# Turned queries laid out by token halves: two transfers per swapped copy in a hybrid attention layer

## The chip, the cores and the metric

The kernel runs on one core of a Trainium2 chip. The metric is the device time of one execution in microseconds (us); times of a kernel are given as the median of several runs. A profile of one execution shows every instruction on the core's engines: PE (TensorE, matmuls; PEld is its weight load), DVE (VectorE), ACT (ScalarE), POOL (GpSimd) and SP (SyncE, which here issues every data transfer, DMA, of the kernel's loop).

## The reference

One encoder layer is applied to two request groups (prompt and sample, 1024 tokens of 1024 channels each) with the same weights. Cut to what matters here:

```python
qa = rms_norm(qa.reshape(B, S, HQ_A, HEAD_DIM), qn_a)      # 8 heads of 64
ka = rms_norm(ka.reshape(B, S, HKV_A, HEAD_DIM), kn_a)     # 2 heads of 64
...                                                        # rotary positions on both
oa = gqa_attention(qa, ka, va) * jax.nn.silu(za)           # branch A: softmax(q k / 8) v

qb = rms_norm(qb.reshape(B, S, H_B, 2, HEAD_DIM), qn_b)    # 4 heads, two maps of 64 each
kb = rms_norm(kb.reshape(B, S, H_B, 2, HEAD_DIM), kn_b)
...
ob = diff_attention(qb, kb, vb, lam)                       # (softmax map 0 - lam * softmax map 1) v
ob = rms_norm(ob, subln_g) * (1.0 - lam_init)
ob = ob.reshape(B, S, BR_B) * jax.nn.silu(zb)

pa = jnp.einsum('bse,ed->bsd', oa, w_proj_a)
pb = jnp.einsum('bse,ed->bsd', ob, w_proj_b)
merged = jax.nn.sigmoid(ga) * pa + jax.nn.sigmoid(gb) * pb
out = jnp.einsum('bsd,de->bse', merged, w_out)
return x + gate[:, None, :] * out                          # gate from c and w_ada
```

## The kernel before

**Numbers in two parts.** TensorE reads rounded float32. A turned query or key (channels on partitions, tokens along the row) is therefore kept as 128 partitions: 64 hold the rounded values, the other 64 what rounding left. A score is the sum of two products: the query as it lies with the key (L743, rounded with rounded and rest with rest), and the query with its two partition halves exchanged (L744, the mixed terms). The exchanged copy is the tile `sw`, which `swapped` (L612 to L620) makes by DMA, since a DMA can move data between partitions. The turning and splitting is `pairs_T` (two transposes on TensorE, L593; ACT writes the rounded half, L595; DVE the rest, L596).

**Units.** Attention works in units of 256 queries (`pr`, the quarter of the tokens) by two score maps: two heads in branch A, the two maps of a head in branch B. A group has 16 units of A (two halves of four heads) and 16 of B, so there are 64. A unit has one `sw` copy and four score steps of 128 queries (`scores`, `softmax_unit`): four matmuls into one of two score banks, the row maximum on DVE (L745), exp on ACT (L746). `flip` then combines the two maps (B only, L786), transposes 32x32 blocks on DVE (L787) and sends the block by four DMAs to the tile `q` (L796, "q<-p" in the profile; the queries themselves are "u" there). The values read `q`: L802 for A, L819 for B. Their output goes to DRAM (L811, L827, "od<-oo").

**Stages of a group.** A head makes A's keys, values and the first half of its queries (`kva_gen`, `qa_gen`), woven with gate columns `z` (L709, written by L722, "zd<-ev"). Then come six phases. In phase 0 attention over A's first half runs beside `qa_gen` of the second; in phase 1 the second half beside B's values and the first B head's queries and keys (`qkb_gen`); in phases 2 to 5 a B head each, beside the next head's `qkb_gen`; the last phase runs beside `gate_gen` (first group only; its eight loads L474 are of 512 KB, into four free 1 MB buffers), the rest of z, and the merge. Merges and the output projection follow.

**What sets the order.** `weave` mixes attention with the fill by hand-set weights; a scheduler then orders each engine's instructions by priorities and its own estimate of when each can start. Attention has a raised priority. A unit's copy `sw` is asked for with the first score steps of the unit before (`attention`, L842 and on), in a pool with two buffers. All DMAs stand in one queue, that of SP, in the order the scheduler gave; their completions rotate over 8 semaphores. Queries, keys, weights and hidden states share 15 buffers of 128 x 2048 numbers (`utile`).

Before the change a unit's queries are two tiles (heads m = 0, 1), each with 1024 tokens for two head pairs; `swapped` has four transfers of 64 partitions x 256 tokens, one for each map and half.

Of the kernel before, what the change touches and what calls it, by code (L numbers as in the profile page):

```python
# [12 lines left out]
F32 = mybir.dt.float32  # L13
F32R = mybir.dt.float32r
# [6 lines left out]
P = 128  # L21
# [67 lines left out]
def kernel(ctx: ExitStack, tc: tile.TileContext, t: dict):  # L89
    nc = tc.nc  # L90
# [36 lines left out]
    def utile():  # L127
        return upool.tile([P, 2048], F32R, tag="u", name=nm("u"))
# [21 lines left out]
    def mtile(tag, shape, dt=F32, bufs=None):  # L150
        return mpool.tile(shape, dt, tag=tag, name=nm(tag), bufs=bufs)
# [4 lines left out]
    dma = nc.sync.dma_start  # L156
# [427 lines left out]
    LO, HI = slice(0, 64), slice(64, 128)  # L584

    def pairs_T(x3, even, odd):


        nb = x3.shape[1] // 2
        ps = gbank()[:, : nb * P].rearrange("p (b n) -> p b n", b=nb)  # L590
        x = x3.rearrange("p (b two) d -> p b (two d)", two=2)
        for b in range(nb):
            nc.tensor.transpose(ps[:, b, :], x[:, b, :], ident)  # L593
        for dst, hi, lo in ((even, LO, HI), (odd, HI, LO)):
            nc.scalar.activation(dst[hi], ps[hi], AF.Copy)  # L595
            nc.vector.tensor_tensor(out=dst[lo], in0=ps[hi], in1=dst[hi].bitcast(F32), op=ALU.subtract)  # L596
# [14 lines left out]

    def swapped(u):  # L612

        qs = u["q"]
        sw = mtile("sw", [P, 2, 256], F32R)[:, : len(qs)]
        sl = slice(u["pr"] * 256, u["pr"] * 256 + 256)
        for m, q in enumerate(qs):
            for a, b in ((LO, HI), (HI, LO)):
                dma(sw[a, m].bitcast(F32), q[b, sl].bitcast(F32))
        return sw  # L620


# [1 line left out]

    def v2(u):
        return u.rearrange("p (h n) -> p h n", h=2)

    def kva_gen(ht, out):
        w = kva_w.pop()[0] if kva_w else load_w(w_cols(w_in, (C_KA, 256)))
# [18 lines left out]

    def qa_gen(st, half):
        w = load_w(w_cols(w_in, (C_QA + half * 256, 256)))  # L650
        qs = [v2(utile()), v2(utile())]
        ht = st["ht"]
        st["qa"][half] = qs

        def front(tt, ps):
            e = by_turns(tt)
            x3, s3 = rms(ps, 4, e)
            e.tensor_tensor(out=x3, in0=x3, in1=gqa.unsqueeze(1).to_broadcast([P, 4, HD]), op=ALU.mult)
            rope(x3, s3, st["cosA"][:, tt], st["sinA"][:, tt], 16, e)
            return x3  # L660

        def back(tt, x3):
            sl = slice(tt * P, (tt + 1) * P)
            pairs_T(x3, qs[0][:, :, sl], qs[1][:, :, sl])
            made[id(qs)] = tt + 1

        yield from pipelined(ht, w, front, back)

    def qkb_gen(ht, out, h):
        w = load_w(w_cols(w_in, (C_QB + h * P, P), (C_KB + h * P, P)))  # L670
        qk = out[h] = (v2(utile()), v2(utile()))

        def front(tt, ps):
            e = by_turns(tt)
            x3, s3 = rms(ps, 4, e)
            x4 = x3.rearrange("p (a m) d -> p a m d", a=2)
            e.tensor_tensor(out=x4, in0=x4, in1=gB.unsqueeze(2).to_broadcast([P, 2, 2, HD]), op=ALU.mult)
            rope(x3[:, :, :16], s3[:, :, :16], cosB[:, tt], sinB[:, tt], 8, e)
            return x3

        def back(tt, x3):
            sl = slice(tt * P, (tt + 1) * P)
            pairs_T(x3, qk[0][:, :, sl], qk[1][:, :, sl])
            made[id(qk)] = tt + 1

        yield from pipelined(ht, w, front, back)
# [50 lines left out]
    def softmax_unit(q, sw, k, pt, su):  # L737

        m = tiny.tile([P, 1], F32, tag="m", name=nm("m"))
        s = sbank()  # L740
        for n in range(2):
            sl = slice(n * 512, (n + 1) * 512)
            nc.tensor.matmul(s[:, sl], q, k[:, sl], start=True, stop=False)  # L743
            nc.tensor.matmul(s[:, sl], sw, k[:, sl], start=False, stop=True)  # L744
        nc.vector.tensor_reduce(out=m, in_=s, axis=AX.X, op=ALU.max, negate=True)  # L745
        nc.scalar.activation(  # L746
            pt.rearrange("p (j c a) -> p j c a", j=4, c=8), s.rearrange("p (c a j) -> p j c a", c=8, j=4),
            AF.Exp, bias=m, accum_out=su,
        )

    def scores(u, i):

        pairs = "h" not in u
        t, m = (i % 2, i // 2) if pairs else (i // 2, i % 2)
        qt = u["pr"] * 2 + t
        if "sw" not in u:
            u["sw"] = swapped(u)
        pt = ptile()
        if pairs:
            su = u["su"][:, m, qt : qt + 1]  # L760
        else:
            su = u["su"][:, qt : qt + 1] if m == 0 else tiny.tile([P, 1], F32, tag="su", name=nm("su"))
        softmax_unit(u["q"][m][:, qt * P : (qt + 1) * P], u["sw"][:, m, t * P : (t + 1) * P], u["k"][m], pt, su)
        if pairs:
            u[m, t] = [pt]
            return m, t
        if m == 0:
            u[t] = [pt]
        else:
            f = tiny.tile([P, 1], F32, tag="r", name=nm("r"))  # L770
            nc.vector.reciprocal(f, su)
            nc.gpsimd.tensor_scalar(
                out=f, in0=f, scalar1=u["su"][:, qt : qt + 1], scalar2=nlam, op0=ALU.mult, op1=ALU.mult
            )
            u[t] += [pt, f]
        return (0, t) if m else None
# [238 lines left out]
    def units_of(st):  # L1015

        def a_unit(half, b, pr):
            kv = half
            j = half * 4 + 2 * b
            return {  # L1020
                "q": [st["qa"][half][i][:, b] for i in range(2)], "k": [st["ka"][:, kv]] * 2,
                "v": st["va"][:, :, kv, :],
                "pr": pr, "od": st["od"][j // 2], "su": st["suA"][:, j : j + 2],
            }

        def b_unit(h, pr):
            qk = st["qkb"][h]
            return {
                "q": [qk[m][:, 0] for m in range(2)], "k": [qk[m][:, 1] for m in range(2)],
                "v": st["vb"][h], "pr": pr, "h": h,  # L1030
                "od": st["od"][4 + h], "ss": st["ssB"], "su": st["suB"][:, h],
            }

        def there(kind, n, pr):
            return made.get(id(st[kind].get(n)), 0) > 2 * pr + 1

        units = []
        for half in range(2):
            units += [
                (half, lambda a=(half, b, pr): a_unit(*a), lambda a=("qa", half, pr): there(*a))  # L1040
                for b in range(2) for pr in range(4)
            ]
        for h in range(4):
            units += [
                (2 + h, lambda a=(h, pr): b_unit(*a), lambda a=("qkb", h, pr): there(*a)) for pr in range(4)
            ]
        return units
# [22 lines left out]
    for g in range(2):  # L1070
        st = states[g]
# [108 lines left out]
```

## Time and profile before

| | before |
|---|---|
| median of 3 runs | 1943.93 us (1940.35 to 1944.71) |
| profiled execution | 1944.48 us |
| its span | 1942.7 us |
| mean granted TensorE clock | 0.987 |
| PE / DVE / ACT / POOL busy | 1867.0 / 1137.7 / 760.3 / 724.5 us |
| `sw` transfers, KB each, median us to landing | 256, 64.0, 2.1 |
| q<-p transfers, KB each, median us to landing | 768, 128.0, 2.6 |

The busy row says how long each engine ran an instruction within the span; DMA issues on SP are not counted in it. A row of the timeline gives start, duration, engine, line, operation, output and inputs with their shape and count; in brackets stands the idle time before it and what ended that. A row of a tile gives the durations as min/median/max in ns and the first and last start. "To landing" is the time from the start of an issue to the completion. The granted clock is the share of full speed that TensorE got.

### The profile page before, as it was taken

Reading aid. Unit: us, or ns where it says so; the run is one execution under the profiler, and the core shown is the slowest. Engines: PE = TensorE matmul, PEld = TensorE weight load, DVE = VectorE, ACT = ScalarE, POOL = GpSimd, SP = SyncE. Lnnn points to the kernel's source line nnn. Section 1 sums busy time; section 2 is a strip of 40 time slices with the busy share of each in tenths; the row PEclk is TensorE's granted clock in tenths of the full one; section 3 lists DMA queues with packets and bytes.
Section 4 is the critical chain, followed back from the end, with each engine's and each line's share of the span. In section 5 each row is a group of like instructions: output and inputs, shape, how many; then the busy total and the mean of one; then the engine's idle time right before and its main releaser. Section 6 shows DMA issues by size and latency. Waiting matters only on the chain. (4 is left out here: it accounts for less than half of the span.)

```text
span 1942.7 us, 29466 instructions
## 1 busy us (share of the span) xinstructions
PE 1867.0 (96%) x10434; PEld 1566.8 (81%) x10434; DVE 1137.7 (59%) x1613; ACT 760.3 (39%) x1548; POOL 724.5 (37%) x1008
## 2 busy tenths in 40 slices
PE   6889999999999998999999899999999999999999
PEld 4777778888888996788888677888888788877887
DVE  5767752444667366757455676445447736666731
ACT  4534442444445344324233444334445534442210
POOL 2564321433456254121336343124456616422110
PEclk9999999999999999999999899999999999999999
DMA  8126774546243355875531567655524423587531
GB/s 315 62 80 166 190 197 129 155 127 201 80 136 102 102 164 155 271 253 187 198 104 51 160 173 195 172 158 152 164 76 139 115 77 93 152 250 251 169 103 54
DMA packets 268882, 295.02 MB, mean 152 GB/s; under 512 B 35136, under 2 KB 217536, under 8 KB 268736
## 3 DMA queue, kind: packets, MB, share of 16 engines
q1 hardware_dynamic: 268736, 293.15, 51.0%
q8 instruction: 83, 1.36, 0.3%
q14 instruction: 63, 0.52, 0.1%
HBM read 133.59 MB, written 42.01 MB: 90 GB/s over the span
## 5 line engine op out<-in xcount | busy, mean ns | idle before, releaser
L709 PE MATMUL f<-u,w 128*128 128x512 f32 x2256 | 588.3, 397 | 2.5 <-ACT w L192 1.0
L709 PEld LDWEIGHTS f<-u,w 128*128 128x128 f32 x2256 | 414.5, 189 | 87.4 <-issue 3.1
L539 PE MATMUL f<-w,u 128*128 128x256 f32 x3456 | 482.4, 285 | 2.4 <-DVE ev L719 1.1
L539 PEld LDWEIGHTS f<-w,u 128*128 128x128 f32 x3456 | 454.6, 191 | 24.7 <-issue 2.7
L745 DVE TENSOR_REDUCE m<-s 128x1 f32<-128x1024 f32 x256 | 310.3, 1217 | 220.3 <-PE s L744 218.2
L746 ACT ACTIVATE p<-s,m 128x1024 f32<-128x1024 f32 x256 | 285.1, 1114 | 290.1 <-DVE m L745 215.2
L194 POOL TENSOR_TENSOR w<-st,w 128x512 fp32r<-128x512 f32 x168 | 222.6, 1342 | 461.3 <-ACT w L192 439.7
L787 DVE STREAM_TRANSPOSE p<-p 128x1024 f32<-128x1024 f32 x192 | 237.7, 1241 | 68.5 <-ACT p L746 56.6
L560 POOL TENSOR_TENSOR rs<-ss,nhalf 128x4 f32<-128x4 f32 (+1 forms) x112 | 111.5, 996 | 312.6 <-DVE ss L559 280.1
L744 PE MATMUL s<-u,sw 128*128 128x512 f32 x512 | 204.7, 401 | 0.0
L192 ACT ACTIVATE w<-st 128x512 fp32r<-128x512 f32 x196 | 114.6, 626 | 148.2 <-DMA st<-in_w_in_dram 92.8
L819 PE MATMUL a<-q,u 128*128 128x256 f32 x512 | 133.8, 396 | 8.1 <-DMA q<-p 5.6
L946 PE MATMUL f<-u,w 128*128 128x512 f32 x552 | 136.8, 398 | 4.0 <-DVE u L957 3.0
L946 PEld LDWEIGHTS f<-u,w 128*128 128x128 f32 x552 | 103.9, 190 | 26.2 <-DVE u L957 3.7
L802 PE MATMUL a<-q,u 128*64 128x256 f32 x1024 | 119.2, 385 | 5.7 <-DMA q<-p 5.7
L819 PEld LDWEIGHTS a<-q,u 128*128 128x128 f32 x512 | 99.5, 200 | 25.6 <-issue 7.0
L743 PE MATMUL s<-u 128*128 128x512 f32 x256 | 108.5, 424 | 10.7 <-ACT p L746 9.9
L596 DVE TENSOR_TENSOR u<-f,u 64x256 fp32r<-64x256 f32 (+1 forms) x196 | 80.6, 411 | 64.4 <-ACT u L595 59.4
L744 PEld LDWEIGHTS s<-u,sw 128*128 128x128 f32 x512 | 97.6, 191 | 17.7 <-issue 0.8
L802 PEld LDWEIGHTS a<-q,u 128*64 128x64 f32 x1024 | 75.3, 138 | 43.9 <-issue 11.4
L743 PE MATMUL s<-u,u 128*128 128x512 f32 x256 | 104.1, 409 | 6.0 <-ACT p L746 4.8
L977 PE MATMUL f<-u,w 128*128 128x512 f32 x456 | 105.6, 389 | 0.0
(169 smaller groups left out, 1984.4 us busy)
## 6 DMA issues: line engine op xcount, KB each, us to landing
q<-p SPq DMA_DIRECT2D x768, 128.0 KB, 2.6
st<-in_w_in_dram SPq DMA_DIRECT2D x132, 256.0 KB, 3.1
zd<-ev SPq DMA_DIRECT2D x96, 256.0 KB, 2.6
sw<-u SPq DMA_DIRECT2D x256, 64.0 KB, 2.1
p<-zd SPq DMA_DIRECT2D x64, 256.0 KB, 3.8
u<-in_w_ada_dram SPq DMA_DIRECT2D x8, 1024.0 KB, 11.6
od<-oo SPq DMA_DIRECT2D x64, 128.0 KB, 2.5
st<-in_w_in_dram SPq DMA_DIRECT2D x64, 128.0 KB, 2.9
```

The lines of the kernel that those rows point to most:

```text
L192: nc.scalar.activation(wh, st, AF.Copy)
L194: e.tensor_tensor(out=wl, in0=st, in1=wh.bitcast(F32), op=ALU.subtract)
L539: ins = nc.tensor.matmul(ps, lt[c][:, sl], w[:, c, wi, :], start=(k == 0), stop=(k == 23))
L709: ins = nc.tensor.matmul(ps, w[:, c, wi, e * P : (e + 1) * P], rt[c], start=(k == 0), stop=(k == 23),)
L743: nc.tensor.matmul(s[:, sl], q, k[:, sl], start=True, stop=False)
L744: nc.tensor.matmul(s[:, sl], sw, k[:, sl], start=False, stop=True)
L745: nc.vector.tensor_reduce(out=m, in_=s, axis=AX.X, op=ALU.max, negate=True)
L746: nc.scalar.activation(pt.rearrange("p (j c a) -> p j c a", j=4, c=8), s.rearrange("p (c a j) -> p j c a", c=8, j=4), AF.Exp, bias=m, accu ...
L787: nc.vector.transpose(pt, pt)
L802: lambda k=k, m=m: nc.tensor.matmul(acc[(LO, HI)[m]], u["v"][:, k], pT[m][:, k], start=(k == 0), stop=(k == 7))
L819: nc.tensor.matmul(acc, u["v"][:, k], pT[:, k], start=(k == 0), stop=(k == 7))
L946: nc.tensor.matmul(ps, w[:, c, wi, d * P : (d + 1) * P], o[:, oi, :], start=(k == 0), stop=(k == 11))
```

## The change

Queries, and B's keys, are now laid out by token halves. `by_tokens` takes the same two buffers, but each holds 512 tokens of both maps, as [partition, head pair b, map m, 512 tokens]; `tokens_of` gives the slices of one 128-token tile to `pairs_T`. In a unit all 256 queries of both maps thus lie in one buffer, and `swapped` moves both maps at once: two transfers of 64 partitions x 2 maps x 256 tokens (128 KB) in place of four of 64 x 256 (64 KB). `softmax_unit` gets the key as a list of two halves of 512 columns, which is how its matmuls already read it. The number of instructions on PE, DVE, ACT and POOL and the buffers stay the same. Line numbers behind L620 shift: L619 to L618, L709 to L714, L743/L744 to L748/L749, L745/L746 to L750/L751, L786/L787 to L792/L793, L796 to L802, L802 to L808, L819 to L825, L827 to L833.

```diff
     def swapped(u):
 
-        qs = u["q"]
-        sw = mtile("sw", [P, 2, 256], F32R)[:, : len(qs)]
-        sl = slice(u["pr"] * 256, u["pr"] * 256 + 256)
-        for m, q in enumerate(qs):
-            for a, b in ((LO, HI), (HI, LO)):
-                dma(sw[a, m].bitcast(F32), q[b, sl].bitcast(F32))
+        sw = mtile("sw", [P, 2, 256], F32R)
+        sl = slice(u["pr"] % 2 * 256, u["pr"] % 2 * 256 + 256)
+        q = u["q"][u["pr"] // 2]
+        for a, b in ((LO, HI), (HI, LO)):
+            dma(sw[a].bitcast(F32), q[b, :, sl].bitcast(F32))
         return sw
...
+    def by_tokens():
+
+        return [utile().rearrange("p (b m n) -> p b m n", b=2, m=2) for _ in range(2)]
+
+    def tokens_of(ts, tt):
+        sl = slice(tt % 4 * P, (tt % 4 + 1) * P)
+        return [ts[tt // 4][:, :, m, sl] for m in range(2)]
...
-        qs = [v2(utile()), v2(utile())]
+        qs = by_tokens()
...
-            sl = slice(tt * P, (tt + 1) * P)
-            pairs_T(x3, qs[0][:, :, sl], qs[1][:, :, sl])
+            pairs_T(x3, *tokens_of(qs, tt))
...
-        qk = out[h] = (v2(utile()), v2(utile()))
+        qk = out[h] = by_tokens()
...
-            sl = slice(tt * P, (tt + 1) * P)
-            pairs_T(x3, qk[0][:, :, sl], qk[1][:, :, sl])
+            pairs_T(x3, *tokens_of(qk, tt))
...
-            nc.tensor.matmul(s[:, sl], q, k[:, sl], start=True, stop=False)
-            nc.tensor.matmul(s[:, sl], sw, k[:, sl], start=False, stop=True)
+            nc.tensor.matmul(s[:, sl], q, k[n], start=True, stop=False)
+            nc.tensor.matmul(s[:, sl], sw, k[n], start=False, stop=True)
...
-                "q": [st["qa"][half][i][:, b] for i in range(2)], "k": [st["ka"][:, kv]] * 2,
+                "q": [x[:, b] for x in st["qa"][half]],
+                "k": [[st["ka"][:, kv, n * 512 : (n + 1) * 512] for n in range(2)]] * 2,
...
-                "q": [qk[m][:, 0] for m in range(2)], "k": [qk[m][:, 1] for m in range(2)],
+                "q": [x[:, 0] for x in qk], "k": [[x[:, 1, m] for x in qk] for m in range(2)],
```

The scheduler gives another order with it. Three places follow. The first is SP's queue in the first group where the gate's loads are issued (L474, `u_...<-in_w_ada_dram`), before:

```order
L827 DMA od_135<-oo_7223 128x256
L474 DMA u_7414<-in_w_ada_dram 128x2x512 x2
L722 DMA zd_7292<-ev_7290 128x512
L796 DMA q_7274<-p_7204 128x1x256 x4
L619 DMA sw_7394<-u_6622 64x256 x2
L619 DMA sw_7394<-u_6623 64x256 x2
L474 DMA u_7434<-in_w_ada_dram 128x2x512 x2
L796 DMA q_7274<-p_7295 128x1x256 x4
L827 DMA od_136<-oo_7359 128x256
L216 DMA st_7630<-in_w_in_dram 128x2x256
```

and now:

```order
L833 DMA od_135<-oo_7167 128x256
L727 DMA zd_7234<-ev_7232 128x512
L802 DMA q_7218<-p_7148 128x1x256 x4
L618 DMA sw_7336<-u_6572 64x2x256 x2
L474 DMA u_7297<-in_w_ada_dram 128x2x512 x2
L474 DMA u_7322<-in_w_ada_dram 128x2x512 x2
L474 DMA u_7354<-in_w_ada_dram 128x2x512 x2
L474 DMA u_7374<-in_w_ada_dram 128x2x512 x2
L802 DMA q_7218<-p_7237 128x1x256 x4
L833 DMA od_136<-oo_7301 128x256
L216 DMA st_7568<-in_w_in_dram 128x2x256
```

Four of the eight loads stood further up still, ahead of the row shown first; all eight are now directly ahead of the four transfers of `p_7237` (`p_7295` before). The second place is DVE in the first group at the second B head, where score units (tiles `s`, maxima `m`) run into one another; before:

```order
L745 TENSOR_REDUCE m_6433<-s_6434 128x1
L771 RECIPROCAL r_6366<-su_6357 128x1
L596 TENSOR_TENSOR u_5533<-f_6015,u_5533 64x2x128
L786 SCALAR_TENSOR_TENSOR p_6298<-p_6356,r_6366,p_6298 128x1024
L745 TENSOR_REDUCE m_6464<-s_6465 128x1
L745 TENSOR_REDUCE m_6502<-s_6503 128x1
L787 STREAM_TRANSPOSE p_6298<-p_6298 128x1024
L596 TENSOR_TENSOR u_5532<-f_6062,u_5532 64x2x128
L771 RECIPROCAL r_6472<-su_6463 128x1
```

and now:

```order
L750 TENSOR_REDUCE m_6385<-s_6386 128x1
L777 RECIPROCAL r_6318<-su_6309 128x1
L596 TENSOR_TENSOR u_5491<-f_5971,u_5491 64x2x128
L750 TENSOR_REDUCE m_6416<-s_6417 128x1
L750 TENSOR_REDUCE m_6452<-s_6453 128x1
L792 SCALAR_TENSOR_TENSOR p_6250<-p_6308,r_6318,p_6250 128x1024
L777 RECIPROCAL r_6424<-su_6415 128x1
L750 TENSOR_REDUCE m_6466<-s_6467 128x1
L793 STREAM_TRANSPOSE p_6250<-p_6250 128x1024
```

The combine `p_6250` moved behind two maxima, and one more maximum, which stood behind the second transpose before, moved ahead of the first; on PE three score units now stand in a row, where two did. The third place is PE in the first group's phase 0, at the values of the fourth unit (tile `a`, the last score unit ahead of it is `s_2434`, now `s_2406`); before:

```order
L593 MATMUL f_2265<-ident,row_1978 128x128 x2
L743 MATMUL s_2434<-u_360,u_900 128x512
L744 MATMUL s_2434<-u_360,sw_2183 128x512
L743 MATMUL s_2434<-u_360,u_900 128x512
L744 MATMUL s_2434<-u_360,sw_2183 128x512
L802 MATMUL a_2321<-q_2282,u_361 64x256
```

and now:

```order
L748 MATMUL s_2406<-u_360,u_899 128x512
L749 MATMUL s_2406<-u_360,sw_2173 128x512
L748 MATMUL s_2406<-u_360,u_899 128x512
L749 MATMUL s_2406<-u_360,sw_2173 128x512
L539 MATMUL f_2176<-w_1410,u_530 128x256
L539 MATMUL f_2176<-w_1410,u_531 128x256
L539 MATMUL f_2176<-w_1410,u_530 128x256 x2
L539 MATMUL f_2176<-w_1410,u_531 128x256
L593 MATMUL f_2253<-ident,row_1970 128x128 x2
L808 MATMUL a_2309<-q_2270,u_361 64x256
```

Another unit's score is what stands just ahead of the values before, and fill work now; the values' own last score lies further up in both.

More of the change, by code (lines that the diff above doesn't have):

```diff
@@ L762, in scores @@
             su = u["su"][:, qt : qt + 1] if m == 0 else tiny.tile([P, 1], F32, tag="su", name=nm("su"))
-        softmax_unit(u["q"][m][:, qt * P : (qt + 1) * P], u["sw"][:, m, t * P : (t + 1) * P], u["k"][m], pt, su)
+        q = u["q"][qt // 4][:, m, qt % 4 * P : (qt % 4 + 1) * P]
+        softmax_unit(q, u["sw"][:, m, t * P : (t + 1) * P], u["k"][m], pt, su)
         if pairs:
```

## The prediction

> **What bounds the kernel now.** I read the page first: busy time, the costliest groups (the maximum and the exp of each score unit, which matter below), DMA issues.
>
> ```profile
> PE 1867.0 (96%) x10434; PEld 1566.8 (81%) x10434; DVE 1137.7 (59%) x1613; ACT 760.3 (39%) x1548; POOL 724.5 (37%) x1008
> ...
> L745 DVE TENSOR_REDUCE m<-s 128x1 f32<-128x1024 f32 x256 | 310.3, 1217 | 220.3 <-PE s L744 218.2
> L746 ACT ACTIVATE p<-s,m 128x1024 f32<-128x1024 f32 x256 | 285.1, 1114 | 290.1 <-DVE m L745 215.2
> ...
> q<-p SPq DMA_DIRECT2D x768, 128.0 KB, 2.6
> ...
> sw<-u SPq DMA_DIRECT2D x256, 64.0 KB, 2.1
> ```
>
> TensorE is busy for 1867.0 of 1942.7 us, so 75.7 us of idle is all that any change outside TensorE can take, and an added wait, or a slower clock behind one, is the only way to lose. The change removes no matmul. So the question is which of TensorE's waits the swapped copies stand behind. I read next what TensorE waited for, per releaser (us in total, times, longest):
>
> ```profile
> PE s L743 <- ACT p L746: 14.7, 8, 3.7
> ...
> PE a L802 <- DMA q<-p: 5.7, 3, 2.5
> PE a L819 <- DMA q<-p: 5.6, 1, 5.6
> ```
>
> No wait names `sw`. The transfers q<-p (turned softmax blocks going to the values) are waited for 11.3 us in four places, and they share SP's queue with `sw`. Then the two tiles' own rows: the 256 `sw` transfers of the run, the 36 between 140 and 300 us, and the q<-p between 200 and 290 us (duration of an issue on SP, min/median/max in ns).
>
> ```profile
> L619 SPq DMA_DIRECT2D sw<-u x256: 461/594/1777, 108.9 to 1713.5; - x128
> ...
> L619 SPq DMA_DIRECT2D sw<-u x36: 468/595/1361, 152.2 to 288.8; - x36
> ...
> L796 SPq DMA_DIRECT2D q<-p x90: 542/602/1657, 199.8 to 287.5; - x90
> ```
>
> SP's timeline shows what this does where branch A's first half runs (start, duration, count):
>
> ```profile
> 212.22 0.52 SPq L619 DMA_DIRECT2D sw<-u  x1
> 212.84 1.21 SPq L796 DMA_DIRECT2D q<-p  x2
> ...
> 214.75 1.19 SPq L796 DMA_DIRECT2D q<-p  x2
> 215.98 0.61 SPq L619 DMA_DIRECT2D sw<-u  x1
> 216.69 1.19 SPq L796 DMA_DIRECT2D q<-p  x2
> 217.93 0.60 SPq L619 DMA_DIRECT2D sw<-u  x1
> 218.58 0.60 SPq L796 DMA_DIRECT2D q<-p  x1
> 219.22 0.60 SPq L619 DMA_DIRECT2D sw<-u  x1
> 219.94 3.16 SPq L796 DMA_DIRECT2D q<-p  x5
> ```
> ```profile
> 211.32 1.25 DVE L787 STREAM_TRANSPOSE p<-p 128x1024 f32<-128x1024 f32 x1 [0.74 <-DMA q<-p]
> ```
> ```profile
> 220.53 0.85 PE L709 MATMUL f<-u,w 128*128 128x512 f32 x3
> 221.22 0.88 PE L539 MATMUL f<-w,u 128*128 128x256 f32 x6
> ...
> 222.86 0.40 PE L744 MATMUL s<-u,sw 128*128 128x512 f32 x1
> 225.51 2.77 PE L802 MATMUL a<-q,u 128*64 128x256 f32 x23 [2.25 <-DMA q<-p]
> ```
>
> SP issues with hardly a gap; four `sw` issues of one unit stand among the q<-p. The block turned at 212.57 gets its issues some 4 us later, and TensorE waits 2.25 us for the last. Here, and in the same stretch of the second group (from 1080 us), SP's queue lies on the path. Last, busy times and clock by stretch:
>
> ```profile
> core 0: us, PE busy (x) PEld busy (x) DVE busy (x) ACT busy (x) POOL busy (x), PEclk, DMA share, GB/s
> 140.00:300.00 160.00, 154.75 (x957) 125.33 (x956) 104.06 (x115) 69.56 (x137) 52.42 (x68) 1.00 0.66 179
> ...
> 1080.00:1240.00 160.00, 156.56 (x932) 126.20 (x932) 104.70 (x116) 70.43 (x139) 54.51 (x71) 0.97 0.67 184
> ```
>
> The two stretches leave 5.25 and 3.44 us idle. Elsewhere q<-p is waited for at one place only, the 5.6 us before L819.
>
> **The change part by part.** *Copies.* Each unit issued 4 × 0.594 = 2.38 us on SP; it now issues two, of 128 row pieces each instead of 64. No row shows a copy of that shape. The nearest is q<-p, also 128 KB from SP, at 0.602. Bounds: 2 × 0.461 (the shortest `sw` row) and 2 × 1.19 (an issue that costs by its rows, nothing saved). I take 2 × 0.62 = 1.24, near q<-p, so 1.1 us a unit: 64 units give about 73 us of SP, 9 units × 1.1 = 10 us in 140–300. Outside the two stretches it lies beside TensorE's work and is worth 0; were that cover gone, it would be 1.1 us a unit.
>
> The Trainium skill ("DMA: Bandwidth & Descriptors", Issuing engines are not separate DMA queues) says that the time a sequencer takes to initiate a DMA is usually small relative to the DMA itself, which speaks against any gain. Here the row has 0.594 us against 2.1 us to landing, and on a full queue the issues add up; by the page's rule the two terms below from SP would be 0.
>
> *Stretch 140–300.* The waits are the 2.25 us above and another of 0.9 (of the 5.7 us under L802, 2.25 and the 2.53 below leave that). The queue gets some 10 us lighter. But the order moves too: counted in the two orders and priced by the spacing of the rows above (0.23 us for a 512-column matmul, 0.12 for a 256-column one), TensorE's work between a unit's last score and its values shrinks for units 3 to 8 from 13.2, 16.3, 20.0, 17.3, 17.5, 16.1 us to 8.9, 11.5, 11.3, 13.9, 14.2, 10.9. Most of what the queue gives is thereby asked back. Bounds: −4.3 (both waits and half of the stretch's other 2.1 us) and +6 (four of the six units reach their values 1.5 us before the data). I take −1.6, half of the waits, because the queue and the order move by like amounts.
>
> *Stall at 1166.* SP, TensorE, and the granted clock of the 3.4 us behind (columns as above):
>
> ```profile
> 1159.85 1.84 SPq L619 DMA_DIRECT2D sw<-u  x3
> 1161.79 5.16 SPq L796 DMA_DIRECT2D q<-p  x8
> ```
> ```profile
> 1166.55 3.82 PE L802 MATMUL a<-q,u 128*64 128x256 f32 x20 [2.53 <-DMA q<-p]
> ```
> ```profile
> 616.50:619.90 3.40, 3.40 (x10) 2.66 (x8) 1.70 (x4) 1.83 (x3) 3.40 (x8) 0.50 0.62 167
> ...
> 1166.00:1169.40 3.40, 2.85 (x14) 2.47 (x16) 2.17 (x4) 0.64 (x3) 2.49 (x4) 0.50 0.65 174
> ```
>
> The values wait for the last of eight q<-p that queue behind three `sw` issues. The pair becomes at most one `sw` issue there: the q<-p goes out some 1.2 us earlier, and half of the 2.53 us stays. A half clock over 3.4 us costs 1.7 us more, and whether it comes hangs on the rest of the gap. Bounds −4.2 (both gone) and 0; I take −2, about the middle.
>
> The Trainium skill ("TensorE: Matmul & The Clock Gate", Part 1) says that the clock is halved after an idle window of some 3.4 us and gaps below some 3 us should keep it warm. The lengths agree (3.4 and 6.8 us at 0.50), but 2.53 us of idle was enough here and 2.25 us at 225 was not. By the page's rule these 1.7 us would not hang on this gap and the term would be −1.2.
>
> *Five score units in a row at 1078.* Two banks hold scores; a third unit waits for the first's maximum (L745, 1.22 us) and exp (L746, 1.11 us).
>
> ```profile
> 1082.93 0.79 PE L743 MATMUL s<-u,u 128*128 128x512 f32 x1 [0.85 <-ACT p L746]
> ```
>
> The new order puts the fifth unit behind two transposes and 24 z matmuls, so 0.85 us of waiting goes, and perhaps part of the half clock there. Bounds −0.85 and −2.6 (with 1.7 of clock), I take −1.7, the middle.
>
> *Three score units in a row at 622.* Before, two came, then z. Now a third follows at once. By the rows of L745 and L746 (1217 and 1114 ns) the first unit's maximum and exp end 2.4 us after its last matmul, while the second unit's scores fill 0.95 us: a wait of about 1.5 us. Behind a wait of that size the half clock may follow, as it did from 616.5 in the row above; at 0.4 times its 1.7 us the term is +2.2, with bounds +1.5 (no slow clock) and +3.4 (a wait of 1.7 and the slow clock).
>
> *Gate loads at 735.* The eight loads of 512 KB for the gate (L474) stood in three places and now follow one another, directly ahead of the q<-p that TensorE waits 5.56 us for:
>
> ```profile
> 727.53 1.12 SPq L474 DMA_DIRECT2D u<-in_w_ada_dram  x2
> 730.57 2.55 SPq L796 DMA_DIRECT2D q<-p  x4
> ```
> ```profile
> 735.46 5.60 PE L819 MATMUL a<-q,u 128*128 128x256 f32 x16 [5.56 <-DMA q<-p]
> 742.07 0.44 PE L593 MATMUL f<-ident,row 128*128 128x128 f32 x2 [1.00 <-POOL row L582]
> ```
> ```profile
> 738.68 1.26 POOL L194 TENSOR_TENSOR w<-st,w 128x512 fp32r<-128x512 f32 x1 [1.33 <-ACT w L192]
> ```
> ```profile
> GB/s 255 101 108 138 93 67 82 164 293 328 405 410 401 306 235 237 198 207 285 123 179 265 205 257 405 194 56 4 0 0 0 69 168 311 4 0 0 0 0 0
> ```
>
> The last row is that of 726 to 745 us; it peaks at 410 GB/s. Eight loads are 4.19 MB, at that rate 10.2 us; issued from about 725.5 (behind the earlier q<-p) they end near 736, and the q<-p, if served behind them, near 737, 1.5 us later than now. Against it: POOL's L194, which held the two transposes behind the values up (1.33 us of waiting, then 1.26), moves behind the rows that they need, so the waits at 742 go, 1.00 us here and 0.3 before the next pair. I take +1.0, not the bare difference of 0.2, because the q<-p's own issue of 0.6 us stands behind the loads too. Bounds: −1 (the q<-p hardly later, the 1.3 us gone) and +8 (the rate of the slices behind the peak, 235 GB/s: 17.8 us, so the loads end at 743.3 and the q<-p 0.6 later, 8.4 us behind now; less 1.3, and half a slow-clock window more).
>
> *Rest.* The four waits for q<-p above are all there are; the other units' data land in time: 0 ± 2.
>
> **Sum**: −1.6 − 2 − 1.7 + 2.2 + 1.0 = −2.1 us against the profiled execution, 1944.48 us (span 1942.7 and 1.8 around it), so 1942.4. That execution lies 0.55 us above the median 1943.93 of the three runs (1940.35 to 1944.71), so I forecast **1941.8 us**: no change that can be measured. About 0.2%, 3.9 us, is what separates runs of this kernel from no change.
>
> **The rivals.**
>
> *A, faster: the queue was the whole cause.* With 73 us less on SP all waits for q<-p in the two stretches go. For it: SP without gaps, three q<-p waits there. Against it: values asked for earlier. −3.7 in 140–300, −4.2 at 1166, −2.2 at 1083, +2.2 at 622, 0 at 735: −7.9, so 1936.
>
> *B, slower: the gate loads.* One mechanism, the loads ahead of the q<-p at 735, with the price +8 of the bound above. The other terms make −3.1, so it is slower by more than 3.9 us from a delay of 3.9 + 3.1 + 1.3 = 8.3 us on, that is if the q<-p lands after 743.8; with +8, and +2.2 to +3.4 at 622, the time is 1948.8 to 1950. For it: the 5.56 us show that this place is already short of data. Against it: 410 GB/s was reached here.
>
> *C, slower: moved values meet the old queue.* If in 140–300 the queue stays as late as it is while the values come 3 to 9 us earlier, the waits grow by up to the shrinks: 4.3 + 4.8 + 8.7 + 3.4 + 3.3 + 5.2 = 29.7 us. A wait at one unit also delays the next unit's request, so they don't add in full; a third to two thirds, +10 to +20, with the other −0.5: 1953 to 1963. Against it: the queue does get lighter.
>
> *D, nothing: the saving isn't there.* If an issue costs by its rows, two copies take what four took (2 × 1.19), the two SP terms fall away and the rest cancels to within 2 us: about 1944. For it: no row has this shape. Against it: q<-p moves twice the bytes of `sw` at the same 0.60 us.
>
> **How the numbers follow.** Forecast and D together 0.40 (0.30 and 0.10), A 0.36 with all that lies between it and 1940, B 0.18, C 0.06. From these: faster 0.36, same 0.40, slower 0.24. The likeliest is the forecast. The range reaches to 1932 (A, and twice the 2 us of the rest) and to 1951 (B, and 1 us of the rest), and leaves C and the far end of A out, under 2 in 10. The forecast's own range is 1938 to 1946: the sum, and about 4 us either way before A or B begins.
>
> **What would show it.** An `sw` issue near 0.62 us and two a unit, SP's busy time down by about 70 us: the copies' step. An idle time of TensorE in 140–300 near 3.6 us instead of 5.25, with a smaller wait at L808 (the old L802): the stretch; more than 5.25, rival C. The wait near 1166 under 1.5 us and no slow clock behind it; no wait near 1083; a wait of about 1.5 us on exp near 624; and a values wait for q<-p near 735 of 6 to 7 us with the transposes following at once. Above 13.9 us there (5.56 + 8.3), rival B. I am wrong if TensorE's idle total (75.7 us) leaves 70 to 80 us, or if a large wait stands at none of these places.

## The result and the profile after

The changed kernel takes 1944.47 us (median of 20 runs, 1940.49 to 1950.97), the kernel before 1940.38 us in 20 runs beside it (1934.27 to 1946.18): ratio 1.0022, 95% interval 1.0012 to 1.0031. It is 4.1 us slower, where I forecast no change. A second measurement of the changed kernel gave 1.0019 (1.0006 to 1.0031).

How small this is, equal programs show: the kernel before, built and timed apart twice, stood at 1.0013 (1.0003 to 1.0023) and at 0.9992 (0.9979 to 1.0004) to itself. Some 0.1% can thus be scatter between builds; the sign rests on two measurements of the changed kernel, its size only roughly. Also, the profiled execution of before that the prediction was made from (1944.48 us) lay 4.1 us above the median of the 20 runs, and the three runs shown then (median 1943.93) 3.5 above it.

The copies do what they should. The page of the changed kernel, and its rows of the tile `sw`, for the whole run and for 140 to 300 us:

```profile
PE 1858.6 (96%) x10434; PEld 1561.4 (80%) x10434; DVE 1133.1 (58%) x1613; ACT 759.3 (39%) x1548; POOL 723.2 (37%) x1008
...
sw<-u SPq DMA_DIRECT2D x128, 128.0 KB, 2.5
```
```profile
L618 SPq DMA_DIRECT2D sw<-u x128: 590/632/1992, 109.5 to 1705.4; - x128
...
L618 SPq DMA_DIRECT2D sw<-u x18: 630/632/1992, 151.8 to 278.0; - x18
```

An issue takes 0.632 us where a smaller one took 0.594, and there are half as many: 1.26 us a unit instead of 2.38, 71 us of SP in all. In branch A's first half TensorE now hardly idles: in 205 to 275 us it was busy for all 70 us, and in 140 to 300 us for 159.24 of the 160 us, where it was busy for 154.75 before:

```profile
core 0: us, PE busy (x) PEld busy (x) DVE busy (x) ACT busy (x) POOL busy (x), PEclk, DMA share, GB/s
205.00:275.00 70.00, 70.00 (x436) 56.01 (x437) 50.08 (x56) 35.05 (x69) 28.19 (x36) 1.00 0.74 206
```
```profile
140.00:300.00 160.00, 159.24 (x984) 129.34 (x983) 106.27 (x119) 71.93 (x141) 52.59 (x68) 1.00 0.66 181
```

What TensorE waited for in the changed kernel (total, times, longest) shows where that gain went:

```profile
PE s L748 <- ACT p L751: 15.4, 7, 3.7
PE f L593 <- POOL row L582: 12.9, 4, 9.6
...
PE f L952 <- DVE u L963: 4.4, 4, 1.7
...
PE a L808 <- DMA q<-p: 2.6, 2, 1.9
```

In the kernel before, the second and third of these lines read:

```profile
PE f L593 <- POOL row L582: 4.3, 5, 2.2
...
PE f L946 <- DVE u L957: 3.0, 2, 1.7
```

The wait for q<-p before L819 (5.6 us) has become one of the transposes L593 for POOL (9.6 us), and the merge's matmuls L952 wait for DVE 4.4 us, where L946 waited 3.0. TensorE's idle total is 1941.5 - 1858.6 = 82.9 us, above the 70 to 80 us beyond which the prediction called itself wrong.

To add this up I counted each matmul at its median spacing in the trace of before (the time from its start to the next one's), and took, for equal TensorE work done, how much more time than work passed: idle plus slow clock, in us per stage (stage ends on the clock of before). Between rows the differences count; the level of a stage depends on the spacings taken. The waits quoted with each experiment are pieces of these sums.

```
stage, us      205-275  600-650  715-762  762-865  1060-1098  1140-1215
before            4.0      4.4      6.9      6.6      11.4       3.7
before, 2nd       5.4      4.5      6.9      4.9       9.3       0.6
before, 3rd       3.0      4.5      6.8      4.4       9.0       0.4
changed          -0.6      6.1      9.8      8.7       9.8       2.5
changed, 2nd     -0.6      6.0      9.8      9.4       9.7       4.5
difference       -4.7     +1.6     +2.9     +3.7      -0.2      +1.9   of the means
```

The six differences make +5.2 us; the medians differ by 4.1. In the first four stages the rows of the two kernels lie apart. In the last two they overlap, so -0.2 and +1.9 are not shown to be differences of the kernels. The second and third profile of before are those of the runs `b_again` and `b_third` below, the second of the changed kernel that of `a_again`.

### The profile page after: what moved, and what is told of

Its sections match the earlier page's. It is cut to its first block, busy times and chain, and to the rows that moved or that the text cites. A ratio compares the mean times of both kernels' runs of the same rounds, so it can differ in the third digit from the quotient of the medians.

```text
span 1941.5 us, 29325 instructions
## 1 busy us (share of the span) xinstructions
PE 1858.6 (96%) x10434; PEld 1561.4 (80%) x10434; DVE 1133.1 (58%) x1613; ACT 759.3 (39%) x1548; POOL 723.2 (37%) x1008
## 5 line engine op out<-in xcount | busy, mean ns | idle before, releaser
L714 PE MATMUL f<-u,w 128*128 128x512 f32 x2256 | 585.7, 396 | 2.5 <-DVE w L194 1.1
L714 PEld LDWEIGHTS f<-u,w 128*128 128x128 f32 x2256 | 412.7, 188 | 86.8 <-issue 3.8
L750 DVE TENSOR_REDUCE m<-s 128x1 f32<-128x1024 f32 x256 | 309.9, 1218 | 220.6 <-PE s L749 218.2
L751 ACT ACTIVATE p<-s,m 128x1024 f32<-128x1024 f32 x256 | 285.1, 1114 | 292.9 <-DVE m L750 221.0
L793 DVE STREAM_TRANSPOSE p<-p 128x1024 f32<-128x1024 f32 x192 | 237.0, 1239 | 65.4 <-ACT p L751 57.7
L749 PE MATMUL s<-u,sw 128*128 128x512 f32 x512 | 204.3, 400 | 0.0
L748 PE MATMUL s<-u,u 128*128 128x512 f32 x384 | 158.7, 414 | 15.1 <-ACT p L751 14.0
L952 PE MATMUL f<-u,w 128*128 128x512 f32 x552 | 136.1, 396 | 7.0 <-DVE u L963 4.4
L825 PE MATMUL a<-q,u 128*128 128x256 f32 x512 | 132.1, 392 | 3.7 <-DMA zd<-ev 1.6
L952 PEld LDWEIGHTS f<-u,w 128*128 128x128 f32 x552 | 102.7, 188 | 30.3 <-DVE u L963 5.9
L808 PE MATMUL a<-q,u 128*64 128x256 f32 x1024 | 117.9, 382 | 2.8 <-DMA q<-p 2.6
L825 PEld LDWEIGHTS a<-q,u 128*128 128x128 f32 x512 | 97.9, 197 | 22.3 <-issue 6.1
L749 PEld LDWEIGHTS s<-u,sw 128*128 128x128 f32 x512 | 97.6, 191 | 17.8 <-issue 0.8
L808 PEld LDWEIGHTS a<-q,u 128*64 128x64 f32 x1024 | 75.2, 137 | 39.9 <-issue 9.5
L792 DVE SCALAR_TENSOR_TENSOR p<-p,r,p 128x1024 f32<-128x1024 f32 x64 | 87.1, 1362 | 26.6 <-POOL r L778 21.1
```

The costliest lines, as they stand in the source:

```text
L714: ins = nc.tensor.matmul(ps, w[:, c, wi, e * P : (e + 1) * P], rt[c], start=(k == 0), stop=(k == 23),)
L748: nc.tensor.matmul(s[:, sl], q, k[n], start=True, stop=False)
L749: nc.tensor.matmul(s[:, sl], sw, k[n], start=False, stop=True)
L751: nc.scalar.activation(pt.rearrange("p (j c a) -> p j c a", j=4, c=8), s.rearrange("p (c a j) -> p j c a", c=8, j=4), AF.Exp, bias=m, accu ...
L793: nc.vector.transpose(pt, pt)
L808: lambda k=k, m=m: nc.tensor.matmul(acc[(LO, HI)[m]], u["v"][:, k], pT[m][:, k], start=(k == 0), stop=(k == 7))
```

## The experiments

My theory once the result was known: the two transfers do gain, in branch A's first half, but the scheduler, given other costs and another layout, derived an order that loses more at a few fixed places. The rival: the larger transfers themselves delay work. The runs came in three groups, each beside the kernel before.

**Both kernels once more** (no edit).

> The kernel before once more, unchanged, for its own scatter and a second profile. In the profiled executions the changed kernel is 1.2 us shorter in span (1941.5 against 1942.7), yet the medians over 20 runs stand the other way (1944.47 against 1940.38). Theory order (the loss comes from where the scheduler put the gate's loads and other instructions) and theory transfers (the larger copies themselves delay work) both expect the ratio 1.000 here, and that the excess of the profiled execution of before (4.1 us over its median) is not found again in one fixed place.

> The changed kernel once more, unchanged: ratio 1.002 to before. Theory order: a second profile again has a TensorE wait of 9 to 10 us near 733 us (transposes L593 waiting for POOL, the values of the unit behind them), against 5.6 + 1.0 + 0.3 us in before, and no wait for q<-p between 220 and 265 us. Theory transfers: waits for sw, or for scores behind sw, stand in this profile in places where before has none.

> The kernel before a third time, for the scatter between equal programs: its second measurement gave 1.0013 [1.0003, 1.0023] against itself. If that was chance, 1.000 here; if a program that is built apart differs by some 0.1%, again 0.999 to 1.0015 outside its interval.

Measured: `b_again` 1943.69 us (1.0013), `a_again` 1943.81 us (1.0019), `b_third` 1937.92 us (0.9992). The places repeat in every profile, the excess of before's first profile does not: its stall of 2.53 us at 1166, with a slow clock behind it, is 0.8 and 0.5 us in the other two. The prediction's term at 1166 was taken from that one stall, and the slow clock in its term at 1078 from the same execution. In `b_again` and in `b_third`:

```profile
1161.23 3.77 PE L802 MATMUL a<-q,u 128*64 128x256 f32 x32 [0.81 <-DMA q<-p]
```
```profile
1158.47 3.77 PE L802 MATMUL a<-q,u 128*64 128x256 f32 x32 [0.50 <-DMA q<-p]
```

In the changed kernel that stage has two waits of 2.6 us in sum, and in its second profile three of 3.1:

```profile
1146.62 3.77 PE L808 MATMUL a<-q,u 128*64 128x256 f32 x32 [0.66 <-DMA q<-p]
1164.30 3.76 PE L808 MATMUL a<-q,u 128*64 128x256 f32 x32 [1.93 <-DMA q<-p]
```

These waits vary by themselves: in the profiles of `merge_order` and `third_unit` below, whose TensorE and SP orders are the same there, they are 4.1 and 1.6 us. No wait for `sw` stands in either profile of the changed kernel.

**Four copies in the new layout.**

```diff
         for a, b in ((LO, HI), (HI, LO)):
-            dma(sw[a].bitcast(F32), q[b, :, sl].bitcast(F32))
+            for m in range(2):
+                dma(sw[a, m].bitcast(F32), q[b, m, sl].bitcast(F32))
```

> The new layout with four transfers of 64 partitions x 256 tokens per unit as before (each map by itself), so SP's issues are those of before and only the layout and the order that the scheduler derives from it differ. The gate's eight loads stand together in SP's queue here as they do in the changed kernel. Theory order: the loss at the gate stays (+2.8 us between 720 and 754 us), the gain of 5 us between 220 and 265 us goes since SP is as loaded as before; so 1944 to 1948 us, slower than before by 0.2 to 0.4%. Theory transfers: without the larger transfer the time is that of before, 1940 to 1941 us, ratio 1.000.

Measured: 1945.07 us, 1.0028 (1.0018 to 1.0037). The layout with its order is slower than before without any larger transfer; the rival as put here is out. The gain between 205 and 275 us is gone (the stage sum is 5.1), and the sum of the gate's stage is 10.3, near the changed kernel's 9.8. In 200 to 270 us TensorE again waits for q<-p:

```profile
PE a L809 <- DMA q<-p: 2.6, 2, 2.0
```

Not all of the excess is found in its profile. The profiled execution (1939.67 us) was the fastest of nine; the second wait for exp near 617 is not in it, nor the changed kernel's loss in the merge: TensorE's waits in 762 to 865 us are 2.0 us in all, against 6.5 in the changed kernel. So the median says that it is slower, and its profile shows only a part of where.

**The gate's loads held behind q<-p.**

```diff
+    turned = [None]            # flip(): turned[0] = dma(dst[:, i, t], ...)
...
-                    dma(wt[:, c : c + 2], rows.rearrange("(c p) n -> p c n", p=P))
+                    behind(dma(wt[:, c : c + 2], rows.rearrange("(c p) n -> p c n", p=P)), turned[0])
```

> The changed kernel with the gate's loads held behind the last q<-p issued before them in the program (an order edge, no wait on the chip), so four transfers q<-p go out ahead of the eight 512 KB loads. Theory order: q<-p lands 2.7 us after its issue instead of 6.7 to 9.2, the wait of 9.57 us near 733 shrinks by 3 us or more, and the time falls by 2.5 to 4 us to 1940.5 to 1942, ratio 1.000 to 1.001. Theory transfers: nothing changes but that place's waits moving to the gate's own matmuls (L324), 1944 us.

Measured: 1958.30 us, 1.0095 (1.0082 to 1.0108). A clear miss. q<-p did land early (2.8 us after its issue at most), and the wait before the values was 5.7 us, that of before. But the sum of the stage 715 to 762 is 21.7 us against 9.8: score units now stand in a row, with four waits for exp (3.3 us), the granted clock is 0.61 from 742 to 765 us, and the last four loads fell behind the next unit's q<-p at 755 us while the gate's matmuls stood in TensorE's order all the same:

```profile
762.71 1.92 PE L324 MATMUL f<-u,cT 128*32 128x512 f32 x4 [2.48 <-DMA u<-in_w_ada_dram]
```

So the loads can be late as well as in the way. That sent me to issue them sooner.

**The first gate loads sooner.** The two first buffers are loaded from within the last head's query and key projection; SP then issues four loads at about 684 us, and the other four at 726 us, behind the q<-p.

```diff
+        def with_gate(gen):
+            for n, step in enumerate(gen):
+                if n == 16:
+                    early.extend(gate_load(0, q) for q in range(2))
+                yield step
...
-                wt = chunks4(utile().bitcast(F32))
-                ...                                  # the two loads
+                wt = early.pop(0) if early else gate_load(half, q)
```

> The changed kernel with the first four of the gate's eight loads given to the scheduler a phase earlier (inside the last head's query and key projection), so they are issued some 20 us ahead and only four loads remain, behind the q<-p instead of ahead of it; the values of that unit stand ahead of the transposes again. Theory order: the 9.57 us wait near 733 becomes 5 to 7 us and the stage from 722 to 754 us costs what it does in before (2.8 us less than in the changed kernel, twice measured); time about 1941.5, ratio 1.000 to 1.001. Theory transfers: no change, 1944, the stage's cost reappears as a wait of the values for q<-p.

Measured: 1935.07 us, 0.9965 (0.9949 to 0.9981). The place is the one, and the gain is larger than I expected (9.4 us by medians against some 3). By the stage sums 3.5 us came at 715 to 762, 2.3 at 762 to 865, and 4.2 at 1140 to 1215, where the edit had moved the second group's order too and no wait for q<-p is left. Only the first of these was aimed at; the rest is luck. Below, the changed kernel's rows at the gate, on TensorE, on SP, and the issue and landing of the four q<-p behind the loads:

```profile
733.77 1.48 PE L593 MATMUL f<-ident,row 128*128 128x128 f32 x4 [9.57 <-POOL row L582]
735.18 3.64 PE L324 MATMUL f<-u,cT 128*32 128x512 f32 x16
738.75 2.43 PE L825 MATMUL a<-q,u 128*128 128x256 f32 x10
```
```profile
721.00 4.40 SPq L474 DMA_DIRECT2D u<-in_w_ada_dram  x8
725.50 4.05 SPq L802 DMA_DIRECT2D q<-p  x4
```
```profile
L802 SPq DMA_DIRECT2D q<-p x4: 542/566/592, 725.5 to 729.0; - x4
...
DMA to landing us min/median/max: 6.7/8.1/9.2
```

The rate from 721 to 735 us in 40 slices, in which the eight loads move, and below it the busy times of the engines from 728.6 to 738.8 us, with the granted clock (0.50), DMA share and rate:

```profile
GB/s 214 144 217 185 94 140 199 334 363 392 421 404 398 416 410 410 386 404 410 415 398 427 392 386 416 416 386 421 410 392 351 328 316 351 363 433 357 386 378 381
```
```profile
728.60:738.80 10.20, 4.92 (x21) 1.23 (x21) 1.69 (x4) 2.14 (x5) 7.02 (x15) 0.50 0.92 336
```

The issue and landing of q<-p in the kernel before, and TensorE's rows in `gate_early`:

```profile
L796 SPq DMA_DIRECT2D q<-p x4: 600/605/611, 730.6 to 732.5; - x4
...
DMA to landing us min/median/max: 2.7/2.7/2.9
```
```profile
729.54 3.72 PE L829 MATMUL a<-q,u 128*128 128x256 f32 x16 [3.03 <-DMA u<-in_w_ada_dram]
737.44 0.44 PE L597 MATMUL f<-ident,row 128*128 128x128 f32 x2 [3.96 <-POOL row L586]
```

In the changed kernel TensorE runs dry at 724.2 us (733.77 less the 9.57 of idle time), and the last q<-p lands at 735.7 (729.0 + 6.7), 11.5 us later. In the kernel before it ran dry at 729.9 and the last landing was at 735.3, 5.4 us later. So behind the eight loads q<-p comes 6.1 us later, as seen from TensorE; the second profile of the changed kernel gives 11.8 us for 11.5. The values could not have begun before that landing, wherever they stood in TensorE's order. The scheduler had put two pairs of transposes and a gate group ahead of them, and these filled a part of the wait: TensorE stood idle 9.57 us, for POOL's rows, and not 11.5, with a granted clock of 0.50 from 728.6 to 738.8.

In `gate_early` the last q<-p lands at 727.7 us, 1.2 us after TensorE runs dry. The values run ahead of POOL's last rows again, and the two waits make 3.03 + 3.96 us, against 9.57. (The row of 3.03 us names a gate load, which landed only at 730.2; for the weight load of the same values the profile names DVE's copy `oo`.)

**Loads ahead in the old layout.** In before, four of the loads are held back to stand ahead of the q<-p:

```diff
-                    dma(wt[:, c : c + 2], rows.rearrange("(c p) n -> p c n", p=P))
+                    behind(dma(wt[:, c : c + 2], rows.rearrange("(c p) n -> p c n", p=P)), turned[-2])
```

> The kernel before with its gate loads held back: the first four loads, which it issues some 30 us ahead, now stand directly ahead of the q<-p of the last unit (four of the eight, the other four behind it). Theory order: the stage from 720 to 755 us loses 2 to 5 us against before, time 1943 to 1946, ratio 1.001 to 1.003, with the old layout and the old copies. Rival (the gate's place costs only together with the new layout's buffers): no change, ratio 1.000.

Measured: 1938.67 us, 0.9992 (0.9983 to 1.0001); no loss, against the 1943 to 1946 expected. q<-p lands up to 6.2 us after its issue and the values wait longer, but the transposes behind them wait no more:

```profile
738.52 5.79 PE L821 MATMUL a<-q,u 128*128 128x256 f32 x16 [8.20 <-DMA q<-p]
```

The stage sum is 8.0 instead of 6.9, with TensorE's order in this stage the same. The last q<-p lands at 738.2 us, 7.9 us after TensorE runs dry, so 2.5 us later than in before; the waits of some 1.3 us behind the values go, and 1.1 us remain. The same working for the changed kernel, 6.1 us later less 1.3, gives 4.8, of which the moved transposes and gate group took 1.9 back (9.57 us idle for 11.5): the 2.9 measured. So eight loads ahead cost more than four because q<-p lands later, not because TensorE's order moved. This is worked out from landings; no run moved TensorE's order alone.

**Three gated products behind the merge products.** DVE's products L919 wait for z to come back from DRAM (q<-zd). In the changed kernel, SP held a z behind two transfers p<-zd that waited for a buffer (1.7 us), and DVE stood still ahead of the merge products. SP, DVE and TensorE of the changed kernel:

```profile
819.44 0.43 SPq L907 DMA_DIRECT2D q<-od  x1
821.14 0.80 SPq L943 DMA_DIRECT2D p<-zd  x2
821.97 0.43 SPq L908 DMA_DIRECT2D q<-zd  x1
```
```profile
826.50 0.75 DVE L919 SCALAR_TENSOR_TENSOR q<-q,subg 128x512 f32<-128x512 f32 x1 [2.51 <-DMA q<-zd]
833.22 0.75 DVE L919 SCALAR_TENSOR_TENSOR q<-q,subg 128x512 f32<-128x512 f32 x1 [3.77 <-DMA q<-zd]
```
```profile
828.57 3.04 PE L952 MATMUL f<-u,w 128*128 128x512 f32 x12 [1.66 <-DVE u L963]
834.62 5.73 PE L952 MATMUL f<-u,w 128*128 128x512 f32 x24 [0.75 <-DVE u L963]
```

```diff
+    LATER = {(2, 1, 0): 4, (3, 0, 1): 4, (3, 1, 0): 5}     # merged: the products L963 in order
...
+                if st is states[0] and (i, hf, c) in LATER:
+                    behind(ins, merged[LATER[i, hf, c]])
```

> The changed kernel with three gated products on VectorE (those whose second factor z has still to come back from DRAM) held behind the fifth and sixth merge product, as they stood in before; no other engine's order moves but for nine matmuls. Theory order: the two waits of TensorE for VectorE's merge products near 828 and 834 us (1.66 and 0.75) go, the stage 807 to 860 us gives 2 to 3 us back, time about 1942, ratio 1.0005. Theory transfers: these waits have another cause and stay; 1944, ratio 1.002.

Measured: 1941.91 us, 1.0000 (0.9986 to 1.0014), 2.6 us below the changed kernel, which was timed in another group; the stage sum falls from 8.7 and 9.4 to 6.4, and the waits for DVE's merge products in 715 to 865 us, 3.1 us before the edit, are

```profile
PE f L957 <- DVE u L968: 1.6, 2, 0.8
```

That is 1.5 us of a loss of 3.7. In the same stage of the changed kernel the values wait 2.7 us for transfers at two places that no experiment aimed at; in before the first is 0.60 us and the second is not there, and here the first is 1.30:

```profile
784.03 1.97 PE L825 MATMUL a<-q,u 128*128 128x256 f32 x8 [1.61 <-DMA zd<-ev]
...
845.16 1.97 PE L825 MATMUL a<-q,u 128*128 128x256 f32 x8 [1.10 <-DMA q<-p]
```

**The third score unit behind z.**

```diff
+            if late and n == 0:
+                behind(ins, zlast[0])        # the last matmul of the z group
```

> The changed kernel with the third of three score units near 617 us held behind the 24 z matmuls, as in before (28 matmuls move). Theory order: the wait of 1.64 us on exp near 617 goes, stage 620 to 650 us gives 1.4 us back, time about 1943. Theory transfers: the score unit meets its wait a few us later instead, no gain, 1944.

Measured: 1942.97 us, 1.0008 (0.9994 to 1.0022), 1.5 us below the changed kernel, which its interval does not separate from it. The second wait is gone, and no other wait stands in its place. The stage sum (6.1 and 6.0) is less sure: in `merge_order`, with both waits in place, the granted clock from 600 to 650 us is 1.00 where it is 0.97 here, so a slow clock that comes or stays away weighs as much as the wait. In 600 to 650 us, the changed kernel and this one:

```profile
PE s L748 <- ACT p L751: 3.6, 2, 2.0
```
```profile
PE s L752 <- ACT p L757: 2.0, 1, 2.0
```

**All three edits, with two copies and with four.** The edits are those of the three runs above; the second kernel has the four transfers of `four_copies` besides.

> The three edits together: gate loads early, merge products and third score unit as in before. Theory order: the three places' costs (2.8 + 3.0 + 1.4 = 7.2 us) go and the gain between 211 and 265 us (4.8 us or more) stays, so 1937 to 1938 us, ratio 0.998, faster than both kernels. Theory transfers: the losses return elsewhere in the same stages, 1942 to 1944.

> The three local edits with four transfers per unit instead of two (new layout kept). What differs from the run with the three edits is the two-transfer copy, with what the scheduler makes of it. Theory order-and-queue (the two transfers themselves gain in branch A's first half, the losses are of the order at three places): the gain of 4.8 us and more between 211 and 265 us goes, 1936 to 1938 us against 1931.3. Rival (the layout, not the transfers, holds the gain): 1931 to 1932.

Measured: with two copies 1931.31 us, 0.9954 (0.9939 to 0.9969), the fastest of all, and faster than the 1937 to 1938 expected, since what `gate_early` gained beyond its aim is in it; with four 1935.26 us, 0.9983 (0.9970 to 0.9995). With the three places mended the two transfers, with the order that comes with them, are worth 4.0 us by the medians of two groups, or 0.29% by the ratios. They gain where they were seen to: the sum of 205 to 275 us is 0.2 against 2.7. In 200 to 270 us, two copies and four:

```profile
PE a L819 <- DMA q<-p: 0.8, 1, 0.8
```
```profile
PE a L820 <- DMA q<-p: 1.8, 1, 1.8
```

**The copies on another queue**, in before, with its four transfers:

```diff
-                dma(sw[a, m].bitcast(F32), q[b, sl].bitcast(F32))
+                nc.scalar.dma_start(sw[a, m].bitcast(F32), q[b, sl].bitcast(F32))
```

> The kernel before with its four copies per unit issued on ScalarE's queue instead of SP's (layout as before; the scheduler's order changes widely). Theory queue (SP's backlog in branch A's first half of each group is what the two transfers relieve): between 211 and 265 us TensorE waits for q<-p no more, the stage gains 4 us or more as in the changed kernel; elsewhere the new order may take or give several us, and ScalarE gets 2.4 us more a unit ahead of its exps, so the total may be slower. Rival (the order of values and scores holds the gain, not SP's load): the waits for q<-p there stay at 2 to 4 us.

Measured: 1934.42 us, 0.9973 (0.9960 to 0.9985), though ScalarE now issues all 256:

```profile
L619 ACTq DMA_DIRECT2D sw<-u x256: 467/494/1610, 109.8 to 1691.3; - x128
```

TensorE has no wait left in 200 to 270 us, and the stage sum is -1.0 against 4.1, the mean of before. The transfers and their bytes are the same; what changed is the queue that issues them, and with it the order, so the run supports the queue as the cause there without isolating it. The Trainium skill ("DMA: Bandwidth & Descriptors", Issuing engines are not separate DMA queues) says that another issuing engine only saves the issuing sequencer's time, usually small against the DMA itself. A single issue is under a third of it here (0.594 us against 2.1 to landing), and in a stage where SP issues without a gap the issues add up: the stage sum fell by about 5 us in 70.

## Why the prediction was wrong

It said no change, 1941.8 us, with a third of the chance on faster; the kernel became 4.1 us slower. Against before it forecast -2.1 us, and the stage sums make +5.2. The size of each term, as the two profiles of the changed kernel and the three of before show it:

- *Copies*: 0.62 us an issue forecast, 0.632 measured; 73 us of SP forecast, 71 measured. Right. Rival D fell with it.
- *Stretch 140–300*: -1.6 forecast, -4.7 measured (205 to 275 us), beyond its bound of -4.3. The step "most of what the queue gives is thereby asked back" failed: TensorE has no wait for q<-p left there though the values come earlier. Rival C fell here.
- *Stall at 1166*: -2 forecast, +1.9 measured on the means, which the scatter of equal orders covers. The step that failed is booking this stall as fixed: with its slow clock it stood in one execution, 3.7 us of loss there, 0.6 and 0.4 in the others, so there was nothing to take. That the changed order loses here, as rival C described, is not shown.
- *Five score units at 1078*: -1.7 forecast, -0.2 measured. The wait of 0.85 did shrink to one of 0.41 on POOL. But the granted clock from 1060 to 1098 us is 0.87 in the first profile of before, 0.96 in its other two and 0.91 in both of the changed kernel: the slow clock that made the term large was that execution's.
- *Three score units at 622*: +2.2 forecast, +1.6 measured (a wait of 1.64). Right in mechanism; the added slow clock didn't come.
- *Gate loads at 735*: +1.0 forecast, +2.9 measured. The mechanism was right and the delay mis-sized: q<-p was put 1.5 us later and came 6.1 us later. The eight loads were priced at 10.2 us; from the first issue to the last landing they took 13.3 (721.0 to 734.3). The rate of 410 GB/s was nearly there (386 to 427 GB/s from 724 to 731 us), but the first load landed only at 725.2, 4.2 us after its issue, and I counted no time before the data flow. The loads also went out about 1.2 us later than I put them, as seen from TensorE. Against that, the order of TensorE, which I took as unchanged, took 1.9 us back. Rival B had the mechanism, not its size: the delay stayed below its 8.3 us.
- *Rest*: 0 ± 2 forecast; the merge at 762 to 865 alone measured +3.7. This is the largest loss, and the step that failed is the term put at nothing: I had looked only at waits for q<-p that stood in before. In the changed kernel DVE waits for z there and TensorE for DVE, and the values wait for zd<-ev and for a q<-p that was in time before.

So two steps turned the sign: the merge's loss was put at nothing, and gains were booked at two places from stalls that one execution happened to have. Without those two gains the sum of the others, as forecast, is +1.6; with the merge's 3.7 it would have come near the result, but only because the errors of the stretch (-3.1) and of the gate (+1.9) partly cancel. It is luck, too, that 1941.8 lies only 2.7 us from 1944.47: the base of three runs was 3.5 us above the median of 20, which hides more than half of the miss.

## What to carry to other kernels

A transfer saved on a full queue is a gain only in the stage where that queue is waited for. Where a scheduler derives the order, every edit also moves other work, and each place where the two orders differ has to be read as such: which engine will stand idle, for which data, and with what work beside it. A burst ahead of a small transfer is priced from its first issue to its last landing, not at its peak rate. Before a stall is booked as a gain, find it in a second execution; and once the moved places are found, mending them one by one turned a loss of 0.2% into a gain of 0.5% here, some of it unaimed.

## What was not expected of the hardware

Issuing a 128 KB copy of 64 partitions with two row pieces took 0.632 us on SP, one of 64 KB with one piece 0.594: the issue hardly grows with the pieces. On ScalarE the small one took 0.494. Eight 512 KB loads issued in 4.4 us made four 128 KB transfers behind them land 6.7 to 9.2 us after their issue, against 2.7 to 2.9 in the kernel before at the same place.
